# A hybrid decoder trunk on one core: the first block sums of pair 1 in each MLP unit, from two DMAs of GpSimd's queue instead of VectorE

## The chip, the core and the metric

The kernel runs on one core of one Trainium2 chip. A core has five engines, each with an instruction stream of its own that it works through in order: TensorE (PE in the profile; its weight loads are PEld), VectorE (DVE), ScalarE (ACT), GpSimd (POOL) and SyncE (SP), which here only issues DMAs. The engines wait for each other by semaphores. The metric is the device time of one execution, in microseconds (us).

## The reference

Two layers. Each maps x (256 tokens x 2048, float32) through a norm and one input projection, two kinds of attention heads, an output projection, and then an MLP whose hidden width is 8192:

```python
hm = rms_norm(x, mlp_norm)
up = jnp.square(jax.nn.relu(jnp.einsum('bsd,df->bsf', hm, w_up)))
return x + jnp.einsum('bsf,fd->bsd', up, w_down)
```

The change touches nothing but these two products of the MLP.

## The kernel before

The matrix products run on TensorE as float32 split in two: each weight block is copied by ScalarE into a high part (`whi`, L984) and VectorE takes the rest as the low part (`wlo`, L988). A product of a block is three matmuls: high by high, high by low and low by high (`product`, L1068, matmul at L1078). Each part is 128 x 1024 numbers (two blocks of 128 x 512), or 128 x 512 where it has only one.

The two products of the MLP are cut into *units*. For each quarter q of the hidden width there are two up units, `("up", q, 0)` and `("up", q, 1)`, then two down units, `("down", q, 0)` and `("down", q, 1)`: 16 units a layer. A unit makes 1024 columns of output for all 256 tokens and runs over 8 *pairs* j = 0 to 7. A pair is 256 rows by 1024 columns of weights, 1 MB, loaded by one DMA of SP (`load`, L924, DMA at L934) into one of four buffers `raw`. The view of it is 2 blocks of rows by 2 blocks of 512 columns.

Most pairs take eight block products, into four banks of PSUM. Pairs 1, 2, 4 and 5 of an up unit and 1, 4 and 5 of a down unit (`FAST`, L414) take seven, as in the scheme of Strassen and Winograd, into seven banks. For those VectorE first has to add blocks of the weights (`steps`, from L1036 on). With w11, w12 (row block 0) and w21, w22 (row block 1):

- `first` (t13, L1040 and L1049): the tile `ts`, 128 x 2 x 512, becomes w11 + w12 and w22 + w12. `ts` has a single buffer.
- t2 (L1050): w12 in `raw` is replaced, in place, by the first half of `ts` plus w22. In the trace this is raw<-ts,raw.
- `fourth` (t4, L1051): the tile `t` (t4) becomes the new w12 plus w21.

All three go through `combine` (L821), so L821 is their line in the trace. Then four groups of parts follow, from the second row block of raw, from t, from ts and from the first row block of raw, each with a high part of ScalarE and a low part of VectorE.

At the end of a unit VectorE puts the banks together (`sums_of`, L1104, and `finals`, L1127; both L821 in the trace, act<-m__...): first three sums for the banks of the extra products, then one final sum for each of the four main banks. After an up unit ScalarE applies scale and ReLU to each result (L1212), and TensorE transposes them. Before a down unit ScalarE seeds each main bank with the running x (`seeds`, L1094, L1100), and this can only be done when that bank's final sum is made. A bank's tile is named m__ with two numbers.

The order is set by a planner (`Plan`). Each step is a piece with an engine, an assumed length, the pieces it depends on and a `lag`. `Plan.run` works out due times backward from TensorE's sequence, and then plays the pieces forward: TensorE and SP take theirs in the order in which they were added, VectorE and ScalarE the ready piece that is due first. The order of this play is the order in which instructions are issued; on the chip each engine keeps to it, whatever the true times are. High and low parts are in a ring of 5, so ScalarE and VectorE can run ahead of TensorE by some parts.

Of the kernel before, what the change touches and what calls it, by code (L numbers as in the profile page):

```python
# [14 lines left out]
ALU = mybir.AluOpType  # L15
AX = mybir.AxisListType

P = 128
# [21 lines left out]
class Plan:  # L40
# [20 lines left out]
    def add(self, engine, length, fn, *deps, lag=0.0):  # L61
        flat = []
        for d in deps:
            flat.extend(d if isinstance(d, (list, tuple)) else [d])
        self.pieces.append(Plan.Piece(engine, length, fn, [d for d in flat if d], lag))
        return self.pieces[-1]

    def run(self):
        t = 0.0
        for p in self.pieces:  # L70
            if p.engine == "PE":
                p.due = t
                t += p.length
        begins = {"DVE": t, "ACT": t}
        unset = {p: len(p.users) for p in self.pieces if p.engine != "PE"}
        last = []

        def settled(p):
            for d in p.deps:
                if d in unset:  # L80
                    unset[d] -= 1
                    if not unset[d]:
                        push(d)

        def push(p):
            end = min([u.due for u in p.users], default=t) - p.lag - self.GAP
            heapq.heappush(last, (-end, -at_of[p], p))

        at_of = {p: i for i, p in enumerate(self.pieces)}
        for p in self.pieces:  # L90
            if p in unset and not p.users:
                push(p)
        for p in reversed(self.pieces):
            if p.engine == "PE":
                settled(p)
        while last:
            end, _, p = heapq.heappop(last)
            p.due = min(-end, begins.get(p.engine, t)) - p.length
            if p.engine in begins:
                begins[p.engine] = p.due  # L100
            settled(p)
        line = {e: [p for p in self.pieces if p.engine == e] for e in ("PE", "SP")}
        free = dict.fromkeys(("PE", "SP", "DVE", "ACT"), 0.0)
        left = {p: len(p.deps) for p in self.pieces}
        at = dict.fromkeys(self.pieces, 0.0)
        ready = {"DVE": [], "ACT": []}
        order, events, count = [], [], 0
        for p in self.pieces:
            if not p.deps:
                events.append((0.0, count, p))  # L110
                count += 1
        came = set()
        while events:
            now, _, p = heapq.heappop(events)
            if p is not None:
                if p.engine in ready:
                    heapq.heappush(ready[p.engine], (p.due, count, p))
                else:
                    came.add(p)
                count += 1  # L120
            for e in free:
                if free[e] > now + 1e-9:
                    continue
                if e in ready:
                    if not ready[e]:
                        continue
                    p = heapq.heappop(ready[e])[2]
                elif line[e] and line[e][0] in came:
                    p = line[e].pop(0)
                else:  # L130
                    continue
                order.append(p)
                free[e] = now + p.length
                heapq.heappush(events, (free[e], count, None))
                count += 1
                for u in p.users:
                    at[u] = max(
                        at[u], free[e] + p.lag + (0.0 if u.engine == e else self.GAP)
                    )
                    left[u] -= 1  # L140
                    if not left[u]:
                        heapq.heappush(events, (at[u], count, u))
                        count += 1
        assert len(order) == len(self.pieces)
        for p in order:
            if p.fn:
                p.fn()
        return max(free.values())
# [3 lines left out]
def trunk_kernel(  # L152
# [17 lines left out]
    nc = tc.nc  # L170
# [51 lines left out]

    ATT = ("v4", "tri", "nones", "ident16", "wg", "reset", "mask16", "lr", "lrT", "ha", "hh", "hl", "hA", "on", "row", "bc")
    MLP = (*(f"{t}{i}" for t in ("whi", "wlo") for i in range(4, 12)), "sxh1", "sxk", "sx1", "sx2", "ts", "t4", "raw2")
    MANUAL = {mybir.EngineType.SP, mybir.EngineType.PE, mybir.EngineType.DVE, mybir.EngineType.Activation}

    def tmp(tag, shape, dt=F32, bufs=2):
        pool = pools["att"] if tag in ATT else pools["mlp"] if tag in MLP else tpool
        return pool.tile(list(shape), dt, tag=tag, name=nm(tag), bufs=bufs)
# [183 lines left out]

    FAST = {"up": (1, 2, 4, 5), "down": (1, 4, 5)}  # L414
    KEPT = 4
    HEAD_KINDS = ("sk", "sv", "gv")
    QUICK = (
        ((5, 6), (5, 6, 7), (5, 6, 7), (5, 6)),
# [389 lines left out]
    def listed(l, front, mixed=None, old=None, linear=None):  # L808
# [7 lines left out]
        add = plan.add  # L816
        MM, TR, V2, V1, A2, A1 = 0.227, 0.108, 1.15, 0.61, 1.0, 0.55
# [5 lines left out]
        def vector(dst, a, b, *deps, op=ALU.add):  # L823
            return add("DVE", V1, lambda: combine(dst(), a(), b(), op), *deps)
# [24 lines left out]
        free = {}  # L849
        whi, wlo, raws = [], [], []  # L850
        part_base = part_turn[0] % 4
        up, done = {}, {}
# [3 lines left out]
        for _ in range(RING):  # L856
            p = add("PE", 0.0 if front else 12 * MM, None)
# [142 lines left out]
        sums13, sums4 = [], []  # L1000


        def steps(u, j, is_fast, r, ld, readers):

            kind, q, _ = units[u]
            op = {
                "gg": hT_now, "o": mixed, "up": hm, "down": up.get(q),
                "sk": hT, "sv": hT, "gv": hT,
            }[kind]

            def blk(k, tt, j=j):
                sl = slice(tt * P, (tt + 1) * P)
                return lambda: (op.t[j][:, k, 0, sl], op.t[j][:, k, 1, sl])

            def ext(i):
                return lambda: (op.x[j][:, i, 0, :], op.x[j][:, i, 1, :])

            if isinstance(ld, dict):
                for c, ms in ((0, (2, 4)), (1, (3, 8))):
                    for k in range(2):  # L1020
                        yield parts(
                            lambda c=c, k=k: r()[:, k : k + 1, c * 512 : (c + 1) * 512],
                            readers, ld[c, k], 1,
                        ), [(m, [(blk(k, tt), 0)]) for tt, m in enumerate(ms)]
                return
            if not is_fast:
                for c, ms in ((0, (2, 4)), (1, (3, 8))):
                    yield parts(
                        lambda c=c: r()[:, :, c * 512 : (c + 1) * 512], readers, ld
                    ), [(m, [(blk(k, tt), k) for k in range(2)]) for tt, m in enumerate(ms)]  # L1030
                return
            box = {}

            def row(k):
                return r()[:, k, :].rearrange("p (c n) -> p c n", c=2)

            def b12():
                return r()[:, 0, 512:]

            def first():  # L1040
                box["13"] = tmp("ts", [P, 2, 512], bufs=1)
                ends = r().rearrange("p k (c n) -> p (k c) n", c=2)[:, ::3, :]
                combine(box["13"], ends, b12().unsqueeze(1).to_broadcast([P, 2, 512]))

            def fourth():
                box["4"] = tmp("t4", [P, 512], bufs=1)
                combine(box["4"], b12(), r()[:, 1, :512])

            t13 = add("DVE", V2, first, ld, sums13[-1] if sums13 else [])  # L1049
            t2 = vector(b12, lambda: box["13"][:, 0, :], lambda: r()[:, 1, 512:], t13)  # L1050
            t4 = add("DVE", V1, fourth, t2, sums4[-1] if sums4 else [])  # L1051
            readers.extend((t13, t2, t4))
            sums13.append([])
            sums4.append([])
            yield parts(lambda: row(1), readers, ld), [
                (2, [(blk(1, 0), 0)]), (3, [(ext(1), 1)]),
            ]
            yield parts(lambda: box["4"].unsqueeze(1), sums4[-1], t4, 1), [
                (4, [(blk(1, 1), 0)]),
            ]  # L1060
            yield parts(lambda: box["13"], sums13[-1], t13), [
                (5, [(ext(3) if op in (hT, hT_now) or kind == "up" and j == KEPT else blk(0, 1), 0)]), (7, [(ext(2), 1)]),
            ]
            yield parts(lambda: row(0), readers, t2), [
                (1, [(blk(0, 0), 0)]), (6, [(ext(0), 1)]),
            ]
# [549 lines left out]
        for u, (kind, q, n2) in enumerate(units):  # L1616
# [13 lines left out]
            begun, p, k = set(), {}, 0  # L1630
            lasts = [j for j in order if j in quick][-1:]
            for j in order:
# [5 lines left out]
                if fine:  # L1638
                    r, ld, readers = load_fine(u, j)
# [276 lines left out]
```

## Time and profile before

| | us |
|---|---|
| median of 3 runs | 2138.92 |
| lowest and highest run | 2138.73, 2139.3 |
| span of the profiled execution | 2137.1 |
| TensorE busy | 2128.5 |
| VectorE busy | 1930.0 |
| ScalarE busy | 1422.7 |
| GpSimd busy | 31.5 |
| DMA engines busy, mean of 16 (SP's queue) | 55.8% |

A row of the list of groups reads: line, engine, operation, output<-input, shape, count | busy us in all, mean ns of one | idle time before them. A row of a timeline reads: start and length in us, engine, line, operation. A row of the list of waits reads: who waited at which line for whom, us in total, times, the longest. Matmuls overlap each other, so a matmul's length in a timeline is more than its share of the time. The trace names tiles without their buffer numbers.

### The profile page before, as it was taken

The page shows a single profiled execution, that of the slowest core. Times are in us where ns is not written, and L with a number is a line of the kernel's source. Part 1 is how long each engine was busy: PE and PEld are TensorE (multiplying, and loading weights), DVE is VectorE, ACT ScalarE, POOL GpSimd, SP SyncE. Part 2 cuts the span into 40 slices and gives each one's busy share as a digit, 9 for nine tenths or more (in the row PEclk, how much of TensorE's full clock was granted, in tenths as well). Part 3 has the DMA queues.
Part 4 walks back from the last instruction along what each step waited for, and adds up shares of the span by engine and source line. Part 5 has one row for each costly group of instructions (what it writes and reads, how often), then busy time and mean ns, then how long its engine had stood idle before and what let it go on. Part 6 is the DMA issues. An engine that isn't in the chain of part 4 may idle for free.

```text
span 2137.1 us, 27196 instructions
## 1 busy us (share of the span) xinstructions
PE 2128.5 (100%) x10114; PEld 1776.4 (83%) x10114; DVE 1930.0 (90%) x2403; ACT 1422.7 (67%) x2101; POOL 31.5 (1%) x57
## 2 busy tenths in 40 slices
PE   9999999999999999999999999999999999999999
PEld 7888888888888888888888988888888888888887
DVE  7977689999999899899999676899999999998997
ACT  7667677666576567566666585876765665765674
POOL 0001000000000000000000010000000000000000
PEclk9999999999999999999999999999999999999999
DMA  7645545565556556555666544556555655564564
GB/s 257 215 146 174 178 177 185 198 211 184 207 196 218 177 197 217 196 193 201 217 206 208 164 155 159 198 190 221 179 210 185 216 180 214 191 223 177 197 211 144
DMA packets 131448, 415.26 MB, mean 194 GB/s; under 512 B 6794, under 2 KB 31954, under 8 KB 131316
## 3 DMA queue, kind: packets, MB, share of 16 engines
q1 hardware_dynamic: 131316, 413.53, 55.8%
q8 instruction: 79, 1.29, 0.2%
q14 instruction: 53, 0.43, 0.1%
HBM read 409.31 MB, written 4.19 MB: 193 GB/s over the span
## 4 chain that ended last, share of the span: by engine, by line
PE 97%; issue 1%; DVE 1%; ACT 1%; DMA 0%; POOL 0%; POOLq 0%
PE acc L634 2%; PE acc L609 1%; PE acc L638 1%; PE acc L612 1%; PE acc L615 1%; PE m__38_167 L1078 1%; PE m__40_173 L1078 0%; PE m__2636_12050 L1078 0%; PE m__596_2644 L1078 0%; PE m__691_3115 L1078 0%; PE m__2731_12521 L1078 0%; PE m__602_2669 L1078 0%; PE m__2642_12075 L1078 0%; PE m__50_207 L1078 0%; PE m__2641_12066 L1078 0%
## 5 line engine op out<-in xcount | busy, mean ns | idle before, releaser
L984 ACT ACTIVATE whi<-raw 128x1024 fp32r<-128x1024 f32 (+1 forms) x706 | 733.8, 1055 | 383.7 <-issue 25.4
L988 DVE TENSOR_TENSOR wlo<-raw,whi 128x1024 fp32r<-128x1024 f32 (+1 forms) x706 | 844.0, 1216 | 27.3 <-ACT whi L984 19.0
L984 ACT ACTIVATE whi<-ts 128x1024 fp32r<-128x1024 f32 x138 | 145.9, 1057 | 113.3 <-PE m__3146_14472 L1078 6.5
L988 DVE TENSOR_TENSOR wlo<-ts,whi 128x1024 fp32r<-128x1024 f32 x138 | 168.8, 1223 | 47.7 <-ACT whi L984 47.6
L821 DVE TENSOR_TENSOR ts<-raw 128x1024 f32<-128x1024 f32 x138 | 168.3, 1219 | 0.6
L593 DVE TENSOR_TENSOR wlo<-raw,whi 128x1024 fp32r<-128x1024 f32 (+2 forms) x80 | 81.3, 1017 | 38.9 <-ACT whi L592 38.2
L984 ACT ACTIVATE whi<-t 128x512 fp32r<-128x512 f32 x138 | 86.2, 625 | 41.7 <-DVE t L821 12.6
L988 DVE TENSOR_TENSOR wlo<-t,whi 128x512 fp32r<-128x512 f32 x138 | 94.6, 685 | 10.0 <-ACT whi L984 9.9
L592 ACT ACTIVATE whi<-raw 128x1024 fp32r<-128x1024 f32 (+2 forms) x80 | 71.1, 889 | 46.0 <-PE acc L615 21.6
L821 DVE TENSOR_TENSOR t<-raw 128x512 f32<-128x512 f32 x138 | 94.7, 686 | 1.2
L821 DVE TENSOR_TENSOR raw<-ts,raw 128x512 f32<-128x512 f32 x138 | 94.5, 685 | 0.4
L634 PE MATMUL acc<-act,whi 128*128 128x512 f32 x256 | 91.9, 400 | 0.0
L638 PE MATMUL acc<-act,wlo 128*128 128x256 f32 x256 | 72.0, 281 | 0.0
L1212 ACT ACTIVATE act<-act,st 128x512 f32<-128x512 f32 x64 | 44.4, 716 | 32.6 <-DVE act L821 32.6
L609 PE MATMUL acc<-whi,act 128*128 128x272 f32 (+2 forms) x192 | 62.8, 327 | 0.0
L612 PE MATMUL acc<-wlo,act 128*128 128x272 f32 (+2 forms) x192 | 61.5, 320 | 0.0
L615 PE MATMUL acc<-whi,act 128*128 128x272 f32 (+2 forms) x192 | 61.4, 320 | 0.0
L634 PEld LDWEIGHTS acc<-act,whi 128*128 128x128 f32 x256 | 48.1, 188 | 10.2
L638 PEld LDWEIGHTS acc<-act,wlo 128*128 128x128 f32 x256 | 48.4, 189 | 0.1
L492 DVE TENSOR_TENSOR act<-act,act 128x512 fp32r<-128x512 f32 x64 | 42.5, 685 | 0.0
L609 PEld LDWEIGHTS acc<-whi,act 128*128 128x128 f32 x192 | 36.4, 190 | 3.6 <-issue 0.7
L488 ACT ACTIVATE act<-act 128x512 fp32r<-128x512 f32 x64 | 39.0, 622 | 0.5
(2819 smaller groups left out, 5771.6 us busy)
## 6 DMA issues: line engine op xcount, KB each, us to landing
raw<-in_w_up_dram SPq DMA_DIRECT2D x128, 1024.0 KB, 4.9
raw<-in_w_down_dram SPq DMA_DIRECT2D x128, 1024.0 KB, 5.4
raw<-in_w_in_dram SPq DMA_DIRECT2D x87, 1024.0 KB, 5.4
raw<-in_w_o_dram SPq DMA_DIRECT2D x32, 1024.0 KB, 5.1
raw<-in_w_in_dram SPq DMA_DIRECT2D x8, 544.0 KB, 3.8
raw<-in_w_in_dram SPq DMA_DIRECT2D x8, 512.0 KB, 3.7
act<-in_x_dram SPq DMA_DIRECT2D x7, 512.0 KB, 8.0
xs<-act SPq DMA_DIRECT2D x4, 512.0 KB, 3.0
```

Source lines behind the costliest of these rows:

```text
L492: nc.vector.tensor_tensor(lo, src, f32(h), ALU.subtract)
L592: newest["hi"] = nc.scalar.activation(hi[:, :, :width], r, AF.Copy).ins
L593: newest["lo"] = nc.vector.tensor_tensor(lo[:, :, :width], r, f32(hi[:, :, :width]), ALU.subtract).ins
L609: nc.tensor.matmul(o, xh[:, sl], whi[:, j, :width], start=(k == 0), stop=False)
L612: nc.tensor.matmul(o, xh[:, sl], wlo[:, j, :width], start=False, stop=False)
L615: nc.tensor.matmul(o, xl[:, sl], whi[:, j, :width], start=False, stop=(k == KT - 1))
L634: nc.tensor.matmul(acc[f], whi[:, j, sl], op.both(k), start=(k == 0), stop=False, skip_group_check=True,)
L638: nc.tensor.matmul(acc[f][:, T:], wlo[:, j, sl], xh, start=False, stop=(k == KT - 1), skip_group_check=True,)
L821: nc.vector.tensor_tensor(dst, a, b, op)
L984: nc.scalar.activation(box["h"][:, :n], src(), AF.Copy)
L988: nc.vector.tensor_tensor(box["l"][:, :n], src(), f32(box["h"][:, :n]), ALU.subtract)
L1212: nc.scalar.activation(box[h][:, tt, :], box[h][:, tt, :], AF.Relu, scale=rr[:, tt : tt + 1],)
```

## The change

In each up and down unit pair 1 (`ADDED`) no longer has its first sums made by VectorE. `ts` is filled from HBM by two DMAs that GpSimd issues: `across` copies w12 into both halves of it, `ends`, which waits for the copy, adds w11 and w22 to what lies there. All other fast pairs keep the sum of VectorE. The sum t2 now waits for `ends` and, by itself, for the load of `raw`, which `first` had waited for until now. The planner gets GpSimd as a third engine whose pieces keep their order, and GpSimd's instructions are issued in the planner's order like the others'.

```diff
-        line = {e: [p for p in self.pieces if p.engine == e] for e in ("PE", "SP")}
-        free = dict.fromkeys(("PE", "SP", "DVE", "ACT"), 0.0)
+        line = {e: [p for p in self.pieces if p.engine == e] for e in ("PE", "SP", "POOL")}
+        free = dict.fromkeys(("PE", "SP", "POOL", "DVE", "ACT"), 0.0)
...
+    ADDED = (1,)
...
-            t13 = add("DVE", V2, first, ld, sums13[-1] if sums13 else [])
-            t2 = vector(b12, lambda: box["13"][:, 0, :], lambda: r()[:, 1, 512:], t13)
+            if kind in ("up", "down") and j in ADDED:
+                def across():
+                    box["13"] = tmp("ts", [P, 2, 512], bufs=1)
+                    nc.gpsimd.dma_start(
+                        box["13"], weights(u, j)[:, 0, 512:].unsqueeze(1).to_broadcast([P, 2, 512])
+                    )
+
+                def ends():
+                    w = weights(u, j)
+                    (row_step, _), (k_step, _), _ = w.ap
+                    nc.gpsimd.dma_start(
+                        box["13"],
+                        bass.AP(
+                            tensor=w.tensor, offset=w.offset,
+                            ap=[[row_step, P], [k_step + 512, 2], [1, 512]],
+                        ),
+                        accum_op=ALU.add,
+                    )
+
+                t13 = add("POOL", 1.2, across, sums13[-1] if sums13 else [], lag=2.5)
+                t13 = add("POOL", 1.2, ends, t13, lag=3.0)
+            else:
+                t13 = add("DVE", V2, first, ld, sums13[-1] if sums13 else [])
+            t2 = vector(b12, lambda: box["13"][:, 0, :], lambda: r()[:, 1, 512:], t13, ld)
```

Of the list `MANUAL`, which gains GpSimd, nothing more is to be seen.

GpSimd's stream, from the end of the attention of layer 0 to the constants of layer 1 (sxh and sxk are tiles of the last attention steps, tri, nones and mask those of the next layer's, named t and mask here). Before:

```order
L1458 MEMSET sxh_620_2769 64x4x64 [waits DVE_49,PE_49,Activation_49]
L1458 MEMSET sxh_628_2801 64x4x64 [waits DVE_49,PE_49,Activation_49]
L1458 MEMSET sxh_669_2980 64x4x64
L1458 MEMSET sxk_3181 64x4x64
L255 MEMSET t_2342_10752 128x128 [waits DVE_49,Activation_49,Pool_49]
L261 MEMSET t_2343_10753 128x128 [waits DMAHW5_49,DMAHW4_49,DMAHW6_49,DMAHW3_49,DMAHW7_49,DMAHW0_49,Activation_49]
```

And the same place in the changed kernel, as far as the third of the 16 units:

```order
L1481 MEMSET sxk_3166 64x4x64
L1053 DMA ts_3744<-in_w_up_dram 128x2x512 [waits DVE_49,Activation_49]
L1060 DMA ts_3744<-in_w_up_dram 128x2x512 [waits DMASW0_49]
L1053 DMA ts_4176<-in_w_up_dram 128x2x512 [waits DMASW1_49,DVE_49,Activation_49]
L1060 DMA ts_4176<-in_w_up_dram 128x2x512 [waits DMASW2_49]
L1053 DMA ts_4557<-in_w_down_dram 128x2x512 [waits DMASW3_49,DVE_49]
L1060 DMA ts_4557<-in_w_down_dram 128x2x512 [waits DMASW4_49]
```

Between the two layers' attention, where GpSimd had no instruction, stand 32 DMAs, a copy (L1053) and an adding one (L1060) for each unit in turn; the copy waits for VectorE, which reads the old `ts`, the adding one for the copy (DMASW is the semaphore of a DMA of GpSimd).

VectorE at the change from the unit `("up", 1, 1)` to `("down", 1, 0)` of layer 0 (raw_5981 and raw_5989 are pair 1 of the down unit, act_6015 and act_6024 hold the first half of the up unit's result, act_6038 and act_6047 the second). Before:

```order
L821 TENSOR_TENSOR act_6038<-act_6015,m__1271_5810 128x1024 [waits DVE_49]
L821 TENSOR_TENSOR ts_6046<-raw_5981 128x1024 [waits DMAHW1_49]
L988 TENSOR_TENSOR wlo_6056<-raw_1302_5938,whi_6032 128x1024 [waits Activation_49]
L821 TENSOR_TENSOR act_6015<-m__1246_5710,t_1318_6003 128x512 [waits DVE_49,PE_49]
L821 TENSOR_TENSOR raw_5981<-ts_6046,raw_5981 128x512 [waits DVE_49]
L821 TENSOR_TENSOR act_6015<-m__1249_5723,act_6015 128x512 [waits PE_49]
L821 TENSOR_TENSOR t_1332_6078<-raw_5981 128x512 [waits DVE_49]
L821 TENSOR_TENSOR act_6038<-m__1256_5748,act_6038 128x512 [waits PE_49]
```

And the same place in the changed kernel:

```order
L822 TENSOR_TENSOR act_6047<-act_6024,m__1271_5818 128x1024 [waits DVE_49]
L822 TENSOR_TENSOR raw_5989<-ts_5973,raw_5989 128x512 [waits DMAHW1_49,DMASW5_49]
L989 TENSOR_TENSOR wlo_6064<-raw_1302_5944,whi_6043 128x1024 [waits Activation_49]
L822 TENSOR_TENSOR t_1330_6072<-raw_5989 128x512 [waits DVE_49]
L822 TENSOR_TENSOR act_6024<-m__1248_5720,t_1319_6012 128x512 [waits PE_49]
L989 TENSOR_TENSOR wlo_1332_6077<-raw_5989,whi_1328_6062 128x1024 [waits Activation_49]
L822 TENSOR_TENSOR act_6024<-m__1250_5731,act_6024 128x512 [waits PE_49]
L822 TENSOR_TENSOR act_6047<-m__1256_5754,act_6047 128x512 [waits PE_49]
```

The sum into ts is gone, the in-place sum t2 stands in its place and waits for two DMAs, the load (DMAHW1) and the adding DMA (DMASW5), and t4 and a low part have moved ahead of the up unit's final sums; before, t2 stood between the final sums of the first and the second bank.

More of the change, by code (lines that the diff above doesn't have):

```diff
@@ L224, in trunk_kernel @@
     MLP = (*(f"{t}{i}" for t in ("whi", "wlo") for i in range(4, 12)), "sxh1", "sxk", "sx1", "sx2", "ts", "t4", "raw2")
-    MANUAL = {mybir.EngineType.SP, mybir.EngineType.PE, mybir.EngineType.DVE, mybir.EngineType.Activation}
+    MANUAL = {mybir.EngineType.SP, mybir.EngineType.PE, mybir.EngineType.DVE, mybir.EngineType.Activation, mybir.EngineType.Pool}
     def tmp(tag, shape, dt=F32, bufs=2):
```

## Prediction

> **What bounds the kernel now.** I read the page of the profile first: its span, the busy times and the chain that ended last.
>
> ```profile
> span 2137.1 us, 27196 instructions
> ...
> PE 2128.5 (100%) x10114; PEld 1776.4 (83%) x10114; DVE 1930.0 (90%) x2403; ACT 1422.7 (67%) x2101; POOL 31.5 (1%) x57
> ...
> PE 97%; issue 1%; DVE 1%; ACT 1%; DMA 0%; POOL 0%; POOLq 0%
> ```
>
> TensorE is busy for 2128.5 of 2137.1 us, so it is idle for 8.6 us in all, and the chain runs through it for 97%. The next view is the list of waits, for TensorE.
>
> ```profile
> PE ps L561 <- POOL ident masks.py:199: 1.5, 1, 1.5
> PE m__38_167 L1078 <- ACT whi L984: 1.4, 1, 1.4
> PE ps L699 <- DVE act L664: 1.3, 2, 0.7
> PE m__38_167 L1078 <- DVE wlo L988: 0.5, 1, 0.5
> ```
>
> These 4.7 us are all that TensorE waits for by name, and none of it lies in an MLP unit: L561 is the warm-up, m__38 is the first bank of the first unit, L699 is in attention. Now two whole MLP units, the second half of an up product and the first half of a down product, in the view of busy times by stretch (PE, PEld, DVE, ACT, POOL, clock, DMA share, GB/s).
>
> ```profile
> 604.00:646.60 42.60, 42.60 (x198) 35.42 (x197) 41.94 (x51) 30.16 (x38) 0.00 (x0) 1.00 0.57 195
> 646.60:690.00 43.40, 43.40 (x202) 36.08 (x201) 42.20 (x50) 31.02 (x40) 0.00 (x0) 1.00 0.56 196
> ```
>
> TensorE is busy for the whole of both stretches, at full clock. VectorE is close behind (41.94 of 42.60), but only behind. So the change can hardly win: it must not make TensorE wait, and that is the whole question.
>
> **What is removed.** The group of the removed instruction:
>
> ```profile
> L821 DVE TENSOR_TENSOR ts<-raw 128x1024 f32<-128x1024 f32 x138 | 168.3, 1219 | 0.6
> ```
>
> There are 16 MLP units in each of two layers, and pair 1 of each goes by seven products: 32 of the 138, 32 x 1.219 = 39.0 us of VectorE. All of it lies beside TensorE at 100%. VectorE is not what ends any wait in an MLP unit, so I count the gain at nothing. The cover is TensorE's own work, and it is not gone when VectorE gets faster.
>
> **What is added, and how long there is for it.** The tile ts has one buffer. The copy into it may start when the last reader of the old ts is done, the low part of pair 5 of the unit before. VectorE must have the sums when it comes to the in-place sum (raw<-ts,raw). The timeline of VectorE before, from the one to the other, at the change from an up to a down unit:
>
> ```profile
> 633.75 1.22 DVE L988 TENSOR_TENSOR wlo<-ts,whi 128x1024 fp32r<-128x1024 f32 x1
> ...
> 635.49 4.62 DVE L988 TENSOR_TENSOR wlo<-raw,whi 128x1024 fp32r<-128x1024 f32 x4
> ...
> 643.55 1.22 DVE L821 TENSOR_TENSOR act<-act,m__1271_5810 128x1024 f32<-128x1024 f32 x1
> 644.68 1.22 DVE L821 TENSOR_TENSOR ts<-raw 128x1024 f32<-128x1024 f32 x1
> 645.82 1.22 DVE L988 TENSOR_TENSOR wlo<-raw,whi 128x1024 fp32r<-128x1024 f32 x1
> 646.95 0.68 DVE L821 TENSOR_TENSOR act<-m__1246_5710,t 128x512 f32<-128x512 f32 x1
> 647.55 0.68 DVE L821 TENSOR_TENSOR raw<-ts,raw 128x512 f32<-128x512 f32 x1
> ```
>
> ts is free at 633.75 + 1.22 = 634.97. By the order of the changed kernel the in-place sum now stands where the removed sum stood, right behind act<-act,m__1271, so VectorE comes to it at 644.68. That leaves 9.7 us. At the next change of unit, down to down, the same two marks are:
>
> ```profile
> 676.84 1.23 DVE L988 TENSOR_TENSOR wlo<-ts,whi 128x1024 fp32r<-128x1024 f32 x1 [0.22 <-ACT whi L984]
> ...
> 688.99 1.22 DVE L821 TENSOR_TENSOR ts<-raw 128x1024 f32<-128x1024 f32 x1
> ```
>
> 688.99 - 678.07 = 10.9 us. Each layer has four units of the tight kind (up to down), 8 places in all; the 24 others I take as 10.9.
>
> When the sums are late, VectorE stands still, since it takes its instructions in order. Queued behind the waiting one are a low part, the sum t4 and the final sums that empty the banks of the old unit. For those wait ScalarE, which scales the result (L1212) and then seeds the bank anew (L1100), and TensorE, which needs that bank. ScalarE and TensorE before:
>
> ```profile
> 647.67 0.72 ACT L1212 ACTIVATE act<-act,st 128x512 f32<-128x512 f32 x1 [1.31 <-DVE act L821]
> 648.30 0.58 ACT L1100 ACTIVATE m__1331_6076<-act 128x512 f32<-128x512 f32 x1
> ```
> ```profile
> 650.54 0.39 PE L1078 MATMUL m__1331_6076<-whi,act 128*128 128x512 f32 x1
> 651.90 0.39 PE L1078 MATMUL m__1333_6088<-whi,act 128*128 128x512 f32 x1
> ```
>
> With the in-place sum starting at s (in steps from start to start, as above: 0.60 for 512 columns, 1.13 for 1024), the second bank's final sum starts after 0.60 + 1.13 + 0.60 (in-place sum, low part, t4), 0.60 (first final) and 1.13 (a low part) more, and ends at s + 4.75; scaling and seeding take 1.25 behind it (647.63 to 648.88 for the first bank). That must be done by 651.90: s may be 645.9, which is 1.2 us of cover. I take it as an upper bound, since VectorE has to make up a lateness in a unit in which it is busy for 42.20 of 43.40 us. So TensorE loses, at each of 8 places, the length of the DMA chain less something between 9.7 and 10.9, and at 24 places less something between 10.9 and 12.1.
>
> **How long the two DMAs take.** The trace has no DMA from POOL and no adding one, so this is bounded from rows of SP's.
>
> ```profile
> raw<-in_w_down_dram SPq DMA_DIRECT2D x128, 1024.0 KB, 5.4
> ...
> raw<-in_w_in_dram SPq DMA_DIRECT2D x8, 512.0 KB, 3.7
> ...
> xs<-act SPq DMA_DIRECT2D x4, 512.0 KB, 3.0
> ```
>
> From below: 3.0 for a copy of 512 KB and 3.7 for the add as if it were a load, 6.7 us. From above, the loads of x in the first 60 us, when DMA was at its fullest:
>
> ```profile
> act<-in_x_dram SPq DMA_DIRECT2D x3, 512.0 KB, 8.3
> ```
>
> 2 x 8.3 = 16.6 us. Between the two I go by the nearest rows: 3.7 for the copy, and for the adding DMA a load of 1 MB, since it has to read the 512 KB in SBUF beside the 512 KB from HBM: 5.4. But it doesn't run alone. The DMA view of 634 to 646 us, just where both would run (first row: GB/s in slices of 0.3 us), and of the two loads that start from 638.5 on in it:
>
> ```profile
> GB/s 246 369 423 314 369 423 423 382 150 27 0 0 150 96 137 123 328 410 355 382 355 396 341 341 219 341 410 382 423 382 396 369 464 314 341 369 382 410 437 369
> DMA packets 964, 3.76 MB, mean 314 GB/s; under 512 B 48, under 2 KB 48, under 8 KB 963
> ...
> raw<-in_w_down_dram SPq DMA_DIRECT2D x2, 1024.0 KB, 7.0
> ```
>
> Three loads of 1 MB run there, at 314 GB/s against 195 for the whole unit, and the later ones already take 7.0 instead of 5.4 us because they share. So 7.0 for the add. For POOL's own work of two issues I take the nearest things that POOL does, a small memset each:
>
> ```profile
> L1858 POOL MEMSET act<- 64x512 f32 x4 | 2.1, 523 | 0.2
> L1458 POOL MEMSET sxh<- 64x256 f32 x6 | 1.7, 308 | 85.2 <-ACT act L793 68.3 <-PE ps L788 16.9
> ```
>
> 0.3 to 0.5 us, 0.8 for two. The chain is 3.7 + 7.0 + 0.8 = 11.5 us, longer than the window.
>
> [...]
>
> **The sum.** With 11.5 us: 8 x (11.5 - 9.7) + 24 x (11.5 - 10.9) = 14.4 + 14.4 = 29 without cover; with the cover of 1.2 us at each place 8 x 0.6 = 5. I take 21, nearer to the first, since the lateness has to be made up by a VectorE with under a microsecond to spare in a unit; it gets back 1.22 at each place, which is why I don't take 29. The gain from VectorE is 0. Other added waits: SP's loads of later pairs need the raw buffer that the in-place sum reads, but that buffer's last reader (the low part of its row 0) is as late only as VectorE is, which is counted. POOL has nothing else to do in these stretches. The profiled execution took 2137.1 us, 1.8 less than the median of the runs, 2138.9; on the median the forecast is 2138.9 + 21 = 2160.
>
> **The rivals.**
> *Hidden.* The chain takes up to 10.3 us and TensorE sees nothing. For it: the lower rows (3.0, 3.7), the 1.2 us of cover, and the gap in the GB/s row, eight slices of at most 150 from 636.4 to 638.8, just when the copy would run. Against it: the three loads behind that gap. 8 x (10.3 - 9.7) = 5 without cover, 0 with it: 2139 to 2143. This is the case on the other side, and it decides at a chain of 10.3 us.
> *Far slower.* The adding DMA moves its bytes at a fraction of a copy's rate, and the chain is over 14.5 us. 8 x 4.8 + 24 x 3.6 = 125 without cover, 86 with it; beyond that each microsecond costs 32. For it: no row shows an adding DMA at all. At 16.6 us: 55 + 137 = 192, so 2331.
> [...]
> *Faster.* A VectorE with 39 us less to do takes something out of TensorE's 8.6 us of idle time. Against it: none of the four waits lies behind a removed sum.
>
> **How the numbers follow.** About 0.2% (4.3 us) is what a measurement of this kernel can tell from no change. Slower as forecast, chain of 10.3 to 14.5 us: 0.50. Hidden: 0.32. Far slower: 0.12. Held up: 0.03. Faster: 0.03. So slower is 0.50 + 0.12 + 0.03 = 0.65, same 0.32, faster 0.03. The predicted time is that of the likeliest, 2160. The range takes in the hidden case and the forecast's own up to a chain of 14.5 us, 2138.9 + some 100 (86 to 125): 2138 to 2240; the forecast alone would be 2143 to 2240. Left out are the far slower, the held up and the faster case, 0.18.
>
> **What would show it.** Right: in the changed kernel's profile VectorE waits at raw<-ts,raw for DMA, 32 times, 0.5 to 3 us each, and TensorE then waits, at the start of a unit, for ScalarE's seeds; the two DMA groups add up to some 11.5 us from issue to landing, the adding one the longer. VectorE's busy time falls by some 39 us either way. Wrong: no wait on the DMAs with a chain under 9.7 us (hidden); or waits and a TensorE that stays at 100% (the cover is larger than I think); or a chain over 14.5 us (far slower); or a time under 2134.6.

## The result and the profile after

| | us |
|---|---|
| before, median of 4 runs | 2138.84 (2138.73 to 2139.3) |
| after, median of 4 runs | 2297.62 (2293.04 to 2301.0) |
| ratio, with its 95% interval | 1.0741 (1.0725 to 1.0757) |

The change makes the kernel 158.8 us slower; 2160 was forecast, in a range up to 2240. The page of the changed kernel, its span, busy times and chain:

```profile
span 2296.6 us, 27315 instructions
...
PE 2187.3 (95%) x10114; PEld 1800.6 (78%) x10114; DVE 1901.0 (83%) x2371; ACT 1421.7 (62%) x2101; POOL 93.9 (4%) x121
...
PE 48%; DVE 23%; DMA 21%; issue 5%; ACT 3%; POOL 0%; ACTq 0%; POOLq 0%; DVEq 0%
```

TensorE carried 97% of the chain before and now 48%; VectorE and the DMAs carry most of the rest. TensorE is idle for 109.3 us instead of 8.6, and with the same 10114 matmuls it is busy for 58.8 us more. VectorE has 29.0 us less to do. The list of waits, VectorE's first, then one of TensorE's at the change from `("up", 1, 1)` to `("down", 1, 0)` of layer 0, the place of the prediction:

```profile
DVE raw L822 <- DMA ts<-in_w_down_dram: 89.2, 16, 6.9
DVE raw L822 <- DMA ts<-in_w_up_dram: 76.6, 16, 7.8
...
PE m__1333_6086 L1101 <- ACT m__1333_6086 L1123: 5.4, 1, 5.4
```

VectorE waits at the in-place sum for the DMAs in all 32 units, 165.8 us in all, 5.2 us each. TensorE then waits for the seed that ScalarE can only make behind VectorE's final sums. The timelines of that place, first VectorE, then GpSimd (start, length, engine, line; in brackets the idle time before and what ended it):

```profile
663.22 1.22 DVE L989 TENSOR_TENSOR wlo<-ts,whi 128x1024 fp32r<-128x1024 f32 x1
...
672.96 1.21 DVE L822 TENSOR_TENSOR act<-act,m__1271_5818 128x1024 f32<-128x1024 f32 x1
680.49 0.69 DVE L822 TENSOR_TENSOR raw<-ts,raw 128x512 f32<-128x512 f32 x1 [6.31 <-DMA ts<-in_w_down_dram]
```
```profile
664.74 0.75 POOL L1053 DMA_DIRECT2D ts<-in_w_down_dram  x1 [40.91 <-DVE wlo L989]
669.20 1.19 POOL L1060 DMA_DIRECT2D ts<-in_w_down_dram  x1 [3.70 <-DMA ts<-in_w_down_dram]
```

The old ts is read at 664.44. The copy is issued at 664.74, the adding DMA at 669.20, behind the copy's landing, and the in-place sum starts at 680.49: the copy with its wait took 4.5 us, the adding DMA 11.3. VectorE was ready at 674.17, 9.7 us after 664.44, which is the window of the prediction to the tenth. The same two DMAs over the whole run, in the view of a single line, the copy (L1053) and then the adding one (L1060):

```profile
DMA to landing us min/median/max: 3.9/4.2/6.5
```
```profile
DMA to landing us min/median/max: 8.5/10.5/11.9
```

The last view is the busy time by stretch of the two units that lie between TensorE's stalls (the same two units as in the prediction), and below them four stretches of 3.41 us, two by two.

```profile
634.90:684.80 49.90, 44.55 (x196) 36.43 (x196) 42.28 (x51) 31.39 (x41) 1.95 (x2) 0.94 0.54 174
684.80:733.40 48.60, 45.94 (x199) 37.44 (x199) 40.80 (x48) 30.41 (x40) 1.94 (x2) 0.95 0.62 211
631.44:634.85 3.41, 1.30 (x6) 0.76 (x5) 2.11 (x4) 0.09 (x1) 0.00 (x0) 1.00 0.99 389
634.85:638.26 3.41, 3.39 (x8) 2.74 (x9) 3.40 (x5) 2.44 (x4) 0.00 (x0) 0.50 0.01 5
587.06:590.47 3.41, 1.51 (x7) 0.93 (x5) 1.26 (x2) 0.00 (x0) 0.00 (x0) 1.00 0.97 380
590.47:593.88 3.41, 2.52 (x10) 1.81 (x11) 3.41 (x6) 1.58 (x2) 0.00 (x0) 1.00 0.10 42
```

The first unit takes 49.90 us instead of 42.60. VectorE works for 42.28 of them and stands before the in-place sum for 6.31: 48.6 of 49.9 are taken. In the second unit it is 40.80 and 4.90 of 48.60. So it is VectorE, with its wait, and not TensorE, that bounds a unit now. The clock column holds something that the prediction had no word for: after a stall TensorE runs at half its clock (0.50 from 634.85 to 638.26).

### The profile page after: what moved, and what is told of

Same layout as the page of the kernel before. It is cut to its first block, busy times and chain, and to the rows that moved or that the text cites. A ratio compares the mean times of both kernels' runs of the same rounds, so it can differ in the third digit from the quotient of the medians.

```text
span 2296.6 us, 27315 instructions
## 1 busy us (share of the span) xinstructions
PE 2187.3 (95%) x10114; PEld 1800.6 (78%) x10114; DVE 1901.0 (83%) x2371; ACT 1421.7 (62%) x2101; POOL 93.9 (4%) x121
## 4 chain that ended last, share of the span: by engine, by line
PE 48%; DVE 23%; DMA 21%; issue 5%; ACT 3%; POOL 0%; ACTq 0%; POOLq 0%; DVEq 0%
DVE wlo L989 12%; DMA ts<-in_w_down_dram 10%; DMA ts<-in_w_up_dram 10%; DVE raw L822 2%; DVE t L822 2%; PE acc L635 2%; DVE ts L822 2%; DVE act L822 2%; ACT whi L985 2%; PE acc L610 1%; PE acc L639 1%; PE acc L613 1%; PE acc L616 1%; DVE act L493 1%; PE m__38_167 L1101 0%
## 5 line engine op out<-in xcount | busy, mean ns | idle before, releaser
L822 DVE TENSOR_TENSOR ts<-raw 128x1024 f32<-128x1024 f32 x106 | 129.5, 1222 | 1.9
L1053 POOL DMA_DIRECT2D ts<-in_w_up_dram x16 | 12.2, 760 | 813.5 <-DVE wlo L989 558.0
L1053 POOL DMA_DIRECT2D ts<-in_w_down_dram x16 | 12.0, 750 | 687.0 <-DVE wlo L989 687.0
```

Of the source, the lines that this page charges most:

```text
L822: nc.vector.tensor_tensor(dst, a, b, op)
```

## The experiments

The theory at the start: the chain of two DMAs, 15.5 us from the copy's issue to the in-place sum, is longer than the window of about 10 us, so VectorE stands still and with it the rest; the adding DMA is slow. The rivals: contention (the added traffic delays the loads), order (t2 and t4 now stand ahead of the final sums), and, on the second DMA, that it is slow by sharing and not by adding.

**e1_copy.** The second DMA copies and doesn't add:

```diff
-                        accum_op=ALU.add,
```

> The second DMA is a plain copy of w11 and w22 (no adding), so ts holds other numbers than the sums; all else is the changed kernel. Theory (the chain of the two DMAs, 15.5 us, is longer than VectorE's window of some 10 us, and the adding DMA with 10.5 us is what makes it so): the second DMA takes 4 to 5 us like the first, the chain is 9 to 10 us, the waits at the in-place sum add up to under 15 us instead of 165.8, and the time is 2139 to 2145. Rival, contention (the extra 1 MB in each unit delays the loads of the weights): the traffic is the same, so about 2298. Rival, order (t2 and t4 ahead of the final sums cost the time): about 2298.

Measured: 2196.81 us, ratio 1.0268 (1.0253 to 1.0283). Its second DMA, in the view of its line:

```profile
DMA to landing us min/median/max: 6.5/7.7/10.1
```

The expectation was wrong: a plain copy at this place takes 7.7 us, not 4 to 5, and VectorE still waits for 72.9 us at the in-place sum. Adding is worth 10.5 - 7.7 = 2.8 us of the chain and some 100 us of the time; more than half of the excess over the first copy's 4.2 is due to something else.

**e2_order.** Two memsets of GpSimd in place of the DMAs:

```diff
-                    nc.gpsimd.dma_start(
-                        box["13"], weights(u, j)[:, 0, 512:].unsqueeze(1).to_broadcast([P, 2, 512])
-                    )
+                    nc.gpsimd.memset(box["13"], 0.0)
...
-                    nc.gpsimd.dma_start(
...
-                        accum_op=ALU.add,
-                    )
+                    nc.gpsimd.memset(box["13"][:, :, :8], 0.0)
```

> The two DMAs are replaced by two memsets of GpSimd into ts (so the sums are left out), with the same pieces, waits and order of all engines. Theory (length of the chain): the chain is some 2 us, nothing waits for it, TensorE stays at 99 to 100% and the time is 2139 to 2142. Rival, order: about 2298, since the order is the same as in the changed kernel. Rival, contention: 2139, so this run does not tell it from the theory.

Measured: 2142.48 us, ratio 1.0015 (1.0005 to 1.0024). The new order, with two short memsets instead of the DMAs, costs some 2 us; it is not the cause.

**e3_own.** A tile of its own for pair 1, so that the copy need not wait for pair 5:

```diff
-    apool = ctx.enter_context(tc.tile_pool(name="acts", bufs=23))
+    apool = ctx.enter_context(tc.tile_pool(name="acts", bufs=22))
...
-                    box["13"] = tmp("ts", [P, 2, 512], bufs=1)
+                    box["13"] = tmp("ts1", [P, 2, 512], bufs=1)
...
-                t13 = add("POOL", 1.2, across, sums13[-1] if sums13 else [], lag=2.5)
+                t13 = add("POOL", 1.2, across, own13[-1] if own13 else [], lag=2.5)
...
```

> Pair 1 gets a tile of its own for its sums (4 KB in each partition, taken from the ring of activations, 22 buffers instead of 23), so its two DMAs wait only for pair 1 of the unit before and can start some 30 us earlier. The same bytes move and the order of the sums is the same. Theory (length of the chain against the window): nothing waits for the DMAs, TensorE is idle for under 15 us, and the time is 2139 to 2143. Rival, contention: about 2298, since the traffic stays. Rival, order: about 2298.

Measured: 2142.29 us, ratio 1.0014 (1.0005 to 1.0023). TensorE and VectorE in its page, and its adding DMA in the view of the line:

```profile
PE 2130.7 (100%) x10114; PEld 1775.3 (83%) x10114; DVE 1903.6 (89%) x2371; ACT 1423.1 (67%) x2101; POOL 94.4 (4%) x121
```
```profile
DMA to landing us min/median/max: 5.8/7.1/8.8
```

The same bytes, the same order, the same two DMAs: no wait for them is left in VectorE's list, and the loss is gone. So it is not the added traffic as such that costs, but where the chain lies and how long it may take. The adding DMA itself is faster here, 7.1 us, and it lies at a place with fewer loads. The DMA view from issue to landing of the adding DMA of the same unit, `("down", 1, 0)` of layer 0, in the changed kernel (11.3 us) and then here (6.1 us; q0 is GpSimd's queue, q1 that of SP's loads; packets, MB, share of the DMA engines):

```profile
q1 hardware_dynamic: 730, 2.81, 68.3%
q0 software_dynamic: 272, 0.52, 25.3%
```
```profile
q0 software_dynamic: 272, 0.52, 55.3%
q1 hardware_dynamic: 150, 0.55, 22.3%
```

Over all 32 units the loads move 1.6 to 3.3 MB (median 2.9) during the adding DMA in the changed kernel, and 0.04 to 2.1 MB (median 1.0) here.

**e4_micro.** DMAs by themselves. The core of it, and its three settings for the pair of DMAs:

```python
def alone(t):
    for n in range(4):
        nc.gpsimd.dma_start(t, pair(n)[:, 0, 512:].unsqueeze(1).to_broadcast([P, 2, 512]))
        nc.gpsimd.dma_start(t, split(pair(n), 512), accum_op=ALU.add)
...
alone(ts)
...
loads(16, 4, ts[:, 0, :8])   # paced by four sums of VectorE each
paced(tp)
...
loads(24, 1, td[:, 0, :8])   # hardly paced
full(td)
```

> None of the computation, only DMAs by themselves: pairs of copy and adding DMA with nothing beside them, beside loads of 1 MB at about 200 GB/s, and beside loads without pause; then plain copies of the same blocks from both queues, and adding DMAs of half, half in one row block, and twice the bytes. Theory (adding is slow by itself): with nothing beside it the adding DMA of 512 KB takes 8 to 11 us where the plain copy takes 3 to 4.5, and twice the bytes take 15 to 20. Rival (it is slow only by sharing the 16 engines with the loads, as my forecast had it): 4 to 5 us with nothing beside it, and 7 to 11 only beside the loads.

Measured, medians from issue to landing: alone the copy takes 4.1 us and the adding DMA 5.7; beside paced loads 7.5 and 8.9. In the hardly paced setting loads ran beside the first two of the four pairs only: there the copy takes 7.4 and 7.5 us and the adding DMA 10.6 and 10.3; in the last two pairs it is 4.3 and 3.9, and 5.9 and 6.1. Plain copies of the added blocks take 4.1 from GpSimd's queue and 3.6 from SP's. Adding half the bytes takes 4.5 (4.1 in one row block). Twice the bytes take 12.5, but loads moved 1.3 to 3.1 MB beside each of these DMAs, so that is no price for adding alone. The theory that adding is slow by itself falls: with nothing beside it, the adding DMA is 1.6 us over the copy. The rival is right in kind; its 4 to 5 us for adding alone was too low.

**e5_wait15, e6_wait12, e7_wait20, e9_wait10.** Chains of memsets as long as wanted, which move nothing over the DMA engines; for 15:

```diff
+                    for _ in range(7):
+                        nc.gpsimd.memset(box["13"], 0.0)
...
+                    for _ in range(8):
+                        nc.gpsimd.memset(box["13"], 0.0)
```

> The two DMAs are replaced by 15 memsets of GpSimd into ts, one after the other (so the sums are left out): a chain as long as that of the changed kernel (some 15 to 15.5 us) that moves nothing over the DMA engines. Theory (only the length of the chain counts): VectorE waits at the in-place sum as in the changed kernel, and the time is 2270 to 2310, with TensorE's clock halved in some 20 to 28 stretches. Rival, contention (the added traffic is what costs): about 2142, as with two memsets. Rival on the clock (it falls because of the DMA traffic and not because TensorE is idle): the clock stays at 1.00 and the time is 2230 to 2245.

> As the run with 15 memsets, with 12: a chain of 12 to 12.5 us, as long as that of the two plain copies. Theory: 2170 to 2205, with 5 to 10 stretches of halved clock. If instead the loss does not follow the length of the chain, it is near the 2142 of the two memsets or near the 2298 of the changed kernel.

> As the run with 15 memsets, with 20: a chain of some 20 us. Theory: 32 places lose about 5 us more each than with 15, some 160 us of idle time more; and since TensorE is then idle for over 2 us at every place, the halved clock takes in all 32 (7 us each, some 220 us at half speed, 110 us lost): 2450 to 2530. If the halved clock did not depend on TensorE's idle time, it would be as often as with 15, and the time some 2440 to 2460.

> As the run with 15 memsets, with 10: a chain of 10.0 to 10.4 us. It tells where the loss begins. With no cover, as in the first line of the sum of the prediction: 8 x 0.3 to 0.7 us, so 2145 to 2148 beside the 2142 of the two memsets. With a cover (the loss so far goes as VectorE's wait for ts less some 20 us, in the runs with 12 and 15 memsets): VectorE waits 3 to 8 us in all, TensorE does not, and the time is 2141 to 2143.

| memsets | time, us | before on that chip, us | loss | VectorE's wait at the in-place sum | mean clock |
|---|---|---|---|---|---|
| 10 | 2143.68 | 2138.90 | 4.8 | 5.6 | 0.999 |
| 12 | 2174.83 | 2139.86 | 35.0 | 55.1 | 1.000 |
| 15 | 2282.99 | 2139.86 | 143.1 | 152.7 | 0.979 |
| 20 | 2465.24 | 2139.86 | 325.4 | 311.2 | 0.944 |

The ratios are 1.0021 (1.0012 to 1.0031) with 10 and 1.0672 (1.0654 to 1.0689) with 15; those with 12 and 20 are single runs. With 15, GpSimd's timeline at the place of above and VectorE's wait:

```profile
660.45 7.04 POOL L1054 MEMSET ts<- 128x1024 f32 x7 [31.88 <-DVE wlo L989]
667.54 8.04 POOL L1058 MEMSET ts<- 128x1024 f32 x8
```
```profile
DVE raw L822 <- POOL ts L1058: 152.7, 32, 6.3
```

A chain of 15.1 us without a byte of traffic gives 143.1 of the 158.8 us, and the halved clock with it (0.979). Counted from the moment ts is free, its chain is 15.3 us long and that of the changed kernel 15.8, which is 16 us over 32 places, as much as the rest of the loss. So the rival contention (loads that come late) falls, and DMA traffic as the cause of the lower clock. With 20 the time is where the theory put it, and TensorE runs at half clock for 2 x 0.056 x 2463.5 = 276 us, more than the 220 expected. Two details of the expectations missed: with 12 there is no stretch of halved clock (mean 1.000), and with 10 the result lies between what cover and no cover would give, so it doesn't tell them apart.

**e8_fill.** The changed kernel, with 280 idle-time matmuls:

```diff
+                    if j == order[0] and kind in ("up", "down") and units[u - 1][0] in ("up", "down") and not p:
+                        def fill(box=box, n=13 if (kind, n2) == ("down", 0) else 8):
+                            t = bank(6)
+                            for _ in range(n):
+                                nc.tensor.matmul(t, box["h"][:, 0, :P], box["h"][:, 0], start=True, stop=True)
+
+                        f = add("PE", 0.0, fill, h, free[6])
+                        free[6] = [f]
+                        whi[-1].append(f)
```

> The changed kernel, with matmuls that nobody reads put ahead of the first product of each unit that follows an MLP unit (13 of 128 x 512 before the first down unit of a quarter, 8 elsewhere, some 0.227 us each, into a bank that is free there), so TensorE works for 1.8 to 2.95 us of each stall instead of standing idle. Theory on the clock (it is halved when TensorE is idle for some 2 us within one of the chip's windows of 3.4 us): nearly all stretches of halved clock go, the stalls of VectorE stay, and the time falls by 35 to 55 us, to 2243 to 2263, though TensorE has 63 us more work. Rival (the clock falls for another reason): the time stays at 2290 to 2300 or gets longer by the added work.

Measured: 2291.58 us (2286.7 to 2298.97), ratio 1.0713 (1.069 to 1.0735), whose interval overlaps that of the changed kernel. The clock by cores, of the changed kernel and then of this one, and this one's busy times and waits:

```profile
core 0: 2296.6 us, clock 0.977
```
```profile
core 0: 2287.4 us, clock 0.992
```
```profile
PE 2230.0 (97%) x10394; PEld 1831.2 (80%) x10394; DVE 1899.3 (83%) x2371; ACT 1419.4 (62%) x2101; POOL 93.9 (4%) x121
...
DVE raw L822 <- DMA ts<-in_w_down_dram: 95.9, 16, 7.3
...
DVE raw L822 <- DMA ts<-in_w_up_dram: 75.7, 16, 8.6
```

A mean clock of 0.977 means 2 x 0.023 x 2296.6 = 106 us at half speed; here it is 2 x 0.008 x 2287.4 = 37. Filling the idle time does keep the clock up, so idleness lowers it. But the time fell by only some 6 us and not by 35 to 55, and its own runs lie further apart than that: that part of the theory was wrong, and the time is the one of the rival, though the rival's reason (the clock falls for something else) is not. By the estimate of 0.227 us each (in the kernel before, six matmuls of 128 x 512 take the 1.36 us from 650.54 to 651.90), TensorE did 280 x 0.227 = 63.6 us more work, and the time did not grow. TensorE has time to spare, because VectorE is what bounds these units; most of what it loses at half speed it would have waited anyway.

**e10_beside.** One DMA of 512 KB started together with 0 to 3 loads of 1 MB:

```python
def beside(t, loads, fn):
    for n in range(4):
...
        for k, raw in enumerate(raws):
            nc.sync.dma_start(raw, pair(8 + 4 * n + k))
        fn(t, n)
```

> None of the computation. An adding DMA of 512 KB, and a plain copy of the same blocks, each started together with 0, 1, 2 and 3 loads of 1 MB from the other queue, four times each. If sharing the DMA engines with the loads makes the second DMA slow: the copy goes from 4.1 us to 7 to 8 and the adding one from 5.7 to 10 to 11 with two or three loads, about a load's own transfer more for each half that goes ahead. If position in the kernel matters in another way (POOL or SBUF busy with other engines), both stay within 2 us of their time alone.

Its DMA issues (last column: median from issue to landing; a to d are 0 to 3 loads):

```profile
adda<-in_w_up_dram POOLq DMA_DIRECT2D x4, 512.0 KB, 5.7
copya<-in_w_up_dram POOLq DMA_DIRECT2D x4, 512.0 KB, 4.0
addb<-in_w_up_dram POOLq DMA_DIRECT2D x4, 512.0 KB, 7.9
copyb<-in_w_up_dram POOLq DMA_DIRECT2D x4, 512.0 KB, 5.7
addc<-in_w_up_dram POOLq DMA_DIRECT2D x4, 512.0 KB, 9.9
copyc<-in_w_up_dram POOLq DMA_DIRECT2D x4, 512.0 KB, 7.9
addd<-in_w_up_dram POOLq DMA_DIRECT2D x4, 512.0 KB, 10.8
copyd<-in_w_up_dram POOLq DMA_DIRECT2D x4, 512.0 KB, 7.7
```

With two or three loads beside them the copy takes 7.7 to 7.9 us and the adding DMA 9.9 to 10.8: the 7.7 of e1_copy and the 10.5 of the changed kernel. VectorE is busy for only 25.9 of 293.9 us in this run, so VectorE is not needed to make the second DMA slow. In the changed kernel the loads move 2.9 MB in the median during the adding DMA, as much as in the setting with three loads; that sharing is enough to explain it. Each of the first two loads adds about 2 us here (5.7, 7.9 and 9.9 for the adding DMA, 4.0, 5.7 and 7.9 for the copy); the third adds 0.9 us to the adding DMA and nothing to the copy.

## Why the prediction was wrong

**The bound and the gain: right.** Taking 38.8 us of sums from VectorE (the group fell from 138 to 106 instructions, 168.3 to 129.5 us) gave nothing; where nothing waits (e2_order, e3_own) the time is within 0.3% of before.

**The window: right.** 9.7 us at all 8 tight places, to the tenth, and 10.8 on average at the 24 others (9.0 to 12.6), for 10.9. With 10 memsets the loss is 4.8 us, some 2 of which the new order costs by itself, with 12 it is 35.0; the 10.3 us at which the prediction let it begin lie between the two.

**The length of the chain: here it failed.** "7.0 for the add" is the term: it took 10.5 us. The copy was 4.2 for 3.7, a small part. The prediction saw that the second DMA meets three loads, and took as its price the 7.0 us that a load of 1 MB takes there. But that is the time of loads which share with each other; an adding DMA of GpSimd's queue that starts into two or three loads takes 9.9 to 10.8 (e10_beside), of which 5.7 is its own. Even a plain copy takes 7.7 there (e1_copy). For adding alone 5.4 was near the 5.7, in part by luck: 5.4 was the median of loads of 1 MB, some of which already share. What sharing adds was taken as 1.6 and is 4.8.

**The sum, with the right chain, holds.** From the copy's issue to the in-place sum it is 15.5 us, the median of the 32. 8 x (15.5 - 9.7) + 24 x (15.5 - 10.9) = 156.8, beside 165.8 of waits and 158.8 of loss. The waits are longer because the copy is issued 0.3 us after ts is free: with 15.8 the sum is 166.4. That the 156.8 lies so near the loss is partly chance, since the loss also holds the cover and the clock, which pull opposite ways. By its condition (a chain over 14.5 us) and its price this is the rival called far slower, which had 0.12: each microsecond was to cost 32 us, so some 160 for the 5 us from 15 to 20 memsets, which cost 182. Its reason was another one, though: an adding DMA that moves its bytes at a fraction of a copy's rate. Alone it takes 5.7 us beside the copy's 4.1; the rest comes from the loads beside it.

**The cover: half of the guess.** Cover is the part of a wait of VectorE that TensorE doesn't feel, since it still has work. At a clock of 1.000 (12 memsets) 55.1 us of waits cost 35.0, so 20.1 us are covered, 0.6 at each place and not 1.2 (0.7 without the 2 us of the new order). In the changed kernel only 165.8 - 158.8 = 7.0 are, in e8_fill, with the clock mostly up, 171.6 - 151.7 = 19.9 again, and with 20 memsets, where some 276 us run at half clock, the loss is 14 us above the waits. So I put some 13 us of the 158.8 down to the halved clock; this is an estimate worked out from these runs, two of them single, and not isolated.

**What would show it.** Waits at raw<-ts,raw 32 times: yes, though of 5.2 us and not 0.5 to 3. TensorE waiting for seeds: yes. The two DMA groups, by their medians: 4.2 + 10.5 = 14.7 us and not 11.5, the adding one the longer as foreseen. VectorE's busy time fell by 29.0 and not 39. The other 10 are no added work: neighbouring instructions of VectorE overlap in the trace (643.55 + 1.22 in the prediction's timeline lies past 644.68), and the busy time counts an overlap once. The lengths of all its instructions, added up one by one, fell by 38.5 us, from 2075.3 to 2036.7. A POOL held up by VectorE, which had 0.03: no, its two issues took 0.75 and 1.19 us while VectorE ran, and 0.73 and 1.21 in e10_beside, where VectorE does hardly anything.

**The clock: missing.** No step of the prediction had it. It is real, but not what made the difference between 2160 and 2298.

What stays open: the 2 us that the new order costs by itself, and why the third load in e10_beside adds less than the first two. A kernel that only keeps the loads away from the adding DMA, with ts left as it is, wasn't tried; e3_own, where fewer loads run beside it, is the nearest.

## What to carry to other kernels

Work moved from an engine to a DMA must be costed as a latency between two marks, from the moment its buffer is free to the moment its reader comes, and that latency at the traffic of that place: here 5.7 us alone became 10.5. When the latency is too long, look at what holds its start: a buffer of its own took the loss away at once, at the same bytes and the same order, though it also gave nothing, because the engine that was relieved wasn't the bound. And once an engine has stalled in order, ask again what bounds the stage: here it was VectorE, so 280 extra matmuls did not make the kernel slower.

## What was not expected of the hardware

In the trace of the changed kernel the granted TensorE clock falls to 0.50 in 23 stretches of 3.41 or 6.83 us, and each of them begins on one and the same grid of 3.41 us. On it 23 windows at full clock hold 1.96 us or more of TensorE's idle time, and the window behind each of them ran at half clock; 9 hold 1.20 to 1.90 us, and behind none of them did the clock fall. The last four rows of the busy times by stretch above lie on that grid: from 631.44 on TensorE was busy for 1.30 of 3.41 us, and the next window ran at 0.50 with 8 matmuls; from 587.06 on it was busy for 1.51, and the next one ran at 1.00, though that idle time lasted for 2.77 us in one piece, across the edge of two windows. So 2.1 us of idle time within one window of the grid was enough here, and 2.77 us across an edge was not.

An adding DMA of 512 KB takes 5.7 us with nothing beside it, 1.6 more than the copy (e4_micro). In the changed kernel it takes 10.5 us in the median: its first packet starts 3.7 to 4.9 us after the issue, and the packets take 6.0 us in the median. The copy's first packet starts 1.45 to 1.6 us after its issue there. How the 4.8 us that the adding DMA takes longer there than alone are shared between the time ahead of its first byte and the transfer was not isolated.
